# Instance norm over 512 channels: 32 units of 4 MB, sums and normalising on VectorE, squares on ScalarE

## The chip, the cores and the metric

The kernel runs on one core of a Trainium2 chip. The time is device time in microseconds (us), from 12 runs of the kernel before; the profile is of one further execution of it.

## The reference

```python
B, G, C_per_g, H, W = 4, 8, 16, 256, 256      # x float32, gamma (G, C_per_g)
mu = x.mean(axis=(3, 4), keepdims=True)
var = ((x - mu) ** 2).mean(axis=(3, 4), keepdims=True)
x_norm = (x - mu) / np.sqrt(var + 1e-5)
out = x_norm * gamma[None, :, :, None, None]
```

There are 4 x 8 x 16 = 512 channels of 65,536 float32 values. Each channel has its own mean and variance, and one of 128 gamma values. Input and output are 134 MB each, and every value has to be read in before its channel's statistics are known.

## The kernel before

A channel is spread over S = 4 partitions, so the 128 partitions hold 32 channels at a time, a unit of 8 MB; there are U = 16 units. A partition's 16,384 values are cut in NCK = 2 tiles of CW = 8,192 values (128 x 8192 float32, 4 MB). The pool `data` has six such tiles, so three units are resident.

`load(u)` (L47) issues two DMAs on SP's queue, one for each tile. `stats(u)` (L90) runs 32 `bn_stats` on VectorE, each over 512 values of a partition (L94). `finalize(u, st)` (L100) turns them into one scale and one shift for each partition: `bn_aggr` (L102), the mean square (L104), a matmul with the matrix `avg`, which averages over the four partitions of a channel (L109), a copy from PSUM (L114), negated mean and variance (L116, L120), the square root on ScalarE (L125), and then reciprocal, scale and shift on VectorE (L127 to L132). `emit(u, scale, shift)` (L135) normalises each tile in place on ScalarE (L138) and issues its write on ScalarE's own DMA queue (L141).

The order is written out by hand: the program runs under a manual schedule, so each engine takes its instructions as the code lists them. Loads 0, 1 and 2 are issued at the start, as far as the six tiles go. The statistics of units 0 and 1 both stand ahead of the first `finalize`:

```python
    st0 = stats(0)
    for u in range(1, U):
        if u + 1 < U:
            tiles[u + 1] = load(u + 1)
        st = stats(u)
        if u == 1:
            emit(0, *finalize(0, st0))
        emit(u, *finalize(u, st))
```

A load into a tile waits until the write of the unit that held the tile has finished. Loads run on the queue that the profile calls q1 or q10, writes on the other; both use the same 16 DMA engines. Before the loop, `gamma` is loaded on ScalarE's queue (L59), repeated over the partitions of each channel (L75), and brought into columns by four small matmuls (L81, L88).

Of the kernel before, what the change touches and what calls it, by code (L numbers as in the profile page):

```python
# [1 line left out]

# [4 lines left out]

F32 = mybir.dt.float32
ALU = mybir.AluOpType
ACTF = mybir.ActivationFunctionType  # L10


@with_exitstack
def kernel(
    ctx: ExitStack,
    tc: tile.TileContext,
    x: bass.AP,
    gamma: bass.AP,
    out: bass.AP,
):  # L20
    nc = tc.nc
    B, G, C, H, W = x.shape
    P = nc.NUM_PARTITIONS
    HW = H * W
    n_ch = B * G * C
    S = 4
    K = P // S
    F = HW // S
    U = n_ch // K
    CW = 8192  # L30
    NCK = F // CW
    FMAX = 512
    NG = (G * C) // K
    assert HW % S == 0 and F % CW == 0 and (G * C) % K == 0

    xv = x.rearrange("b g c h w -> (b g c h w)").rearrange("(u p f) -> u p f", p=P, f=F)
    ov = out.rearrange("b g c h w -> (b g c h w)").rearrange("(u p f) -> u p f", p=P, f=F)
    gv = gamma.rearrange("g c -> (g c)")

    data = ctx.enter_context(tc.tile_pool(name="data", bufs=3 * NCK))  # L40
    singles = ctx.enter_context(tc.tile_pool(name="singles", bufs=1))
    stats_pool = ctx.enter_context(tc.tile_pool(name="stats", bufs=2))
    psum = ctx.enter_context(tc.tile_pool(name="psum", bufs=2, space=bass.MemoryType.PSUM))

    ctx.enter_context(tc.manual_schedule())

    def load(u):  # L47
        ts = []
        for j in range(NCK):
            t = data.tile([P, CW], F32, name="xt")  # L50
            nc.sync.dma_start(out=t[:], in_=xv[u, :, j * CW : (j + 1) * CW])  # L51
            ts.append(t)
        return ts

    tiles = {0: load(0), 1: load(1)}


    g_row = singles.tile([1, G * C], F32, name="g_row")
    nc.scalar.dma_start(out=g_row[:], in_=gv[None, :])  # L59
    eps_t = singles.tile([P, 1], F32, name="eps_t")  # L60
    nc.vector.memset(eps_t[:], 1e-5)  # L61
    avg = singles.tile([P, K, S], F32, name="avg")
    nc.gpsimd.memset(avg[:], 1.0 / S)  # L63
    nc.gpsimd.affine_select(  # L64
        out=avg[:], in_=avg[:], pattern=[[-S, K], [0, S]], compare_op=ALU.is_ge,
        fill=0.0, base=0, channel_multiplier=1,
    )
    nc.gpsimd.affine_select(  # L68
        out=avg[:], in_=avg[:], pattern=[[S, K], [0, S]], compare_op=ALU.is_ge,
        fill=0.0, base=S - 1, channel_multiplier=-1,  # L70
    )
    one = singles.tile([1, 1], F32, name="one")
    nc.vector.memset(one[:], 1.0)
    g_rep = singles.tile([1, NG, K, S], F32, name="g_rep")
    nc.vector.tensor_copy(  # L75
        out=g_rep[:],
        in_=g_row[:].rearrange("o (n k) -> o n k", n=NG).unsqueeze(3).to_broadcast([1, NG, K, S]),
    )
    g_ps = psum.tile([P, NG], F32, name="g_ps")
    for n in range(NG):  # L80
        nc.tensor.matmul(  # L81
            out=g_ps[:, n : n + 1],
            lhsT=g_rep[:, n].rearrange("o k s -> o (k s)"),
            rhs=one[:],
            start=True, stop=True,
        )
    g_col = singles.tile([P, NG], F32, name="g_col")
    nc.vector.tensor_copy(out=g_col[:], in_=g_ps[:])  # L88

    def stats(u):  # L90
        st = stats_pool.tile([P, F // FMAX, 6], F32, name="st")
        for j in range(NCK):
            for s in range(CW // FMAX):
                nc.vector.bn_stats(  # L94
                    out=st[:, j * (CW // FMAX) + s, :],
                    in_=tiles[u][j][:, s * FMAX : (s + 1) * FMAX],
                )
        return st

    def finalize(u, st):  # L100
        mv = stats_pool.tile([P, 2], F32, name="mv")
        nc.vector.bn_aggr(out=mv[:], in_=st[:].rearrange("p n s -> p (n s)"))  # L102

        nc.vector.scalar_tensor_tensor(  # L104
            out=mv[:, 1:2], in0=mv[:, 0:1], scalar=mv[:, 0:1], in1=mv[:, 1:2],
            op0=ALU.mult, op1=ALU.add,
        )
        ps = psum.tile([P, 2], F32, name="ps")
        nc.tensor.matmul(  # L109
            out=ps[:], lhsT=avg[:].rearrange("p k s -> p (k s)"), rhs=mv[:],  # L110
            start=True, stop=True,
        )
        cm = stats_pool.tile([P, 2], F32, name="cm")
        nc.vector.tensor_copy(out=cm[:], in_=ps[:])  # L114
        nmean = stats_pool.tile([P, 1], F32, name="nmean")
        nc.vector.tensor_scalar(  # L116
            out=nmean[:], in0=cm[:, 0:1], scalar1=-1.0, scalar2=None, op0=ALU.mult,
        )
        var = stats_pool.tile([P, 1], F32, name="var")
        nc.vector.scalar_tensor_tensor(  # L120
            out=var[:], in0=cm[:, 0:1], scalar=nmean[:], in1=cm[:, 1:2],
            op0=ALU.mult, op1=ALU.add,
        )
        std = stats_pool.tile([P, 1], F32, name="std")
        nc.scalar.activation(out=std[:], in_=var[:], func=ACTF.Sqrt, bias=eps_t[:], scale=1.0)  # L125
        rstd = stats_pool.tile([P, 1], F32, name="rstd")
        nc.vector.reciprocal(out=rstd[:], in_=std[:])  # L127
        scale = stats_pool.tile([P, 1], F32, name="scale")
        g = u % NG
        nc.vector.tensor_mul(out=scale[:], in0=rstd[:], in1=g_col[:, g : g + 1])  # L130
        shift = stats_pool.tile([P, 1], F32, name="shift")
        nc.vector.tensor_mul(out=shift[:], in0=nmean[:], in1=scale[:])  # L132
        return scale, shift

    def emit(u, scale, shift):  # L135
        for j in range(NCK):
            t = tiles[u][j]
            nc.scalar.activation(  # L138
                out=t[:], in_=t[:], func=ACTF.Identity, bias=shift[:], scale=scale[:],
            )  # L140
            nc.scalar.dma_start(out=ov[u, :, j * CW : (j + 1) * CW], in_=t[:])  # L141


    st0 = stats(0)
    for u in range(1, U):
        if u + 1 < U:
            tiles[u + 1] = load(u + 1)
        st = stats(u)
        if u == 1:
            emit(0, *finalize(0, st0))  # L150
        emit(u, *finalize(u, st))
        del tiles[u - 1]


# [1 line left out]
_INS = ['x', 'gamma']  # L156
_OUTS = [((4, 8, 16, 256, 256), 'float32')]


# [23 lines left out]
```

## Time and profile before

| what | value |
|---|---|
| median of 12 runs | 634.72 us (634.19 to 635.17) |
| the profiled execution's own time | 635.17 us |
| its span, first to last instruction | 633.5 us |
| VectorE busy | 343.2 us, 54% |
| ScalarE busy | 236.8 us, 37% |
| TensorE busy | 11.2 us, 2% |
| moved by DMA | 268.50 MB, mean 424 GB/s over the span |

The span is what the instructions of the profile cover; the execution's own time lies 1.67 us above it. Busy shares are averages over the whole span. The view of groups gives for each kind of instruction its busy time, the mean of one in ns, and the idle time of its engine just before it with what ended it. A DMA has an issue on a queue, which is short, and a landing, which is later: loads took 26.9 us from issue to landing in the median, writes 50.7 us.

### The profile page before, as it was taken

How to read it: one execution, taken by the hardware profiler on the slowest of the kernel's cores; microseconds unless marked ns; L12 is line 12 of the kernel's file. 1: busy time of each engine (PE TensorE's matmuls, PEld its weight loads, DVE VectorE, ACT ScalarE, POOL GpSimd, SP SyncE). 2: the span in 40 equal slices, each digit the busy share in tenths (PEclk: the TensorE clock that was granted, in tenths of full speed). 3: DMA queues.
4: the chain of work that ended last, by engine and by line, in shares of the span. 5: the costliest groups of instructions: out<-in, count | busy, mean ns of one | idle time of the engine just before them, and what ended most of it. 6: DMA issues, size and time to landing. Idle time of an engine off the chain costs nothing.

```text
span 633.5 us, 972 instructions
## 1 busy us (share of the span) xinstructions
PE 11.2 (2%) x40; PEld 9.8 (2%) x40; DVE 343.2 (54%) x644; ACT 236.8 (37%) x49; POOL 1.4 (0%) x7
## 2 busy tenths in 40 slices
PE   1000000000000000000000000000000000000000
PEld 1000000000000000000000000000000000000000
DVE  2995496454765536664366653467535575354700
ACT  0004959053170622607135080440904408054180
POOL 0000000000000000000000000000000000000000
DMA  9997999999999999999999999999999999999996
GB/s 379 435 441 335 397 424 432 430 430 429 430 435 430 430 430 437 445 435 433 428 430 432 430 435 430 431 432 437 443 432 430 432 432 431 432 432 430 430 430 272
DMA packets 9225, 268.50 MB, mean 424 GB/s; under 512 B 1025, under 2 KB 1026, under 8 KB 1026
## 3 DMA queue, kind: packets, MB, share of 16 engines
q1 hardware_dynamic: 4608, 134.22, 49.3%
q10 hardware_dynamic: 4610, 134.22, 49.3%
q14 instruction: 7, 0.06, 0.0%
HBM read 134.22 MB, written 134.22 MB: 424 GB/s over the span
## 4 chain that ended last, share of the span: by engine, by line
DMA 56%; DVE 20%; another core or an unknown queue 12%; ACT 7%; PE 1%; issue 1%; SPq 0%; ACTq 0%
DMA xt<-in_x_dram 40%; DVE st L94 17%; DMA out_dram<-xt 15%; ACT xt L138 7%; DVE mv L102 2%; PE ps L109 1%; SPq L51 0%; DVE mv L104 0%; ACT std L125 0%; DVE var L120 0%; DVE cm L114 0%; DVE nmean L116 0%; DVE rstd L127 0%; ACTq L141 0%
## 5 line engine op out<-in xcount | busy, mean ns | idle before, releaser
L94 DVE BATCH_NORM_STATS2 st<-xt 128x6 f32<-128x512 f32 x512 | 306.8, 677 | 220.3 <-DMA xt<-in_x_dram 220.1
L138 ACT ACTIVATE xt<-xt,shift,scale 128x8192 f32<-128x8192 f32 x32 | 230.8, 7213 | 16.7 <-DVE shift L132 9.9
L125 ACT ACTIVATE std<-var,eps_t 128x1 f32<-128x1 f32 x16 | 4.7, 294 | 360.5 <-DVE var L120 360.0
L109 PE MATMUL ps<-mv,avg 128*128 128x2 f32 x32 | 9.4, 362 | 585.0 <-DVE mv L104 585.0
L109 PEld LDWEIGHTS ps<-mv,avg 128*128 128x128 f32 x32 | 8.0, 311 | 586.4 <-DVE mv L104 536.7
L102 DVE BATCH_NORM_AGGREGATE mv<-st 128x2 f32<-128x192 f32 x16 | 16.3, 1020 | 0.5
L127 DVE RECIPROCAL rstd<-std 128x1 f32<-128x1 f32 x16 | 2.6, 163 | 18.6 <-ACT std L125 18.6
L114 DVE COPY cm<-ps 128x2 f32<-128x2 f32 x16 | 2.5, 159 | 10.9 <-PE ps L109 10.9
L120 DVE SCALAR_TENSOR_TENSOR var<-cm,nmean 128x1 f32<-128x1 f32 x16 | 3.5, 220 | 0.6
L104 DVE SCALAR_TENSOR_TENSOR mv<-mv 128x1 f32<-128x1 f32 x16 | 3.5, 219 | 0.6
L132 DVE TENSOR_TENSOR shift<-nmean,scale 128x1 f32<-128x1 f32 x16 | 2.6, 160 | 0.6
L130 DVE TENSOR_TENSOR scale<-rstd,g_col 128x1 f32<-128x1 f32 x16 | 2.5, 159 | 0.5
L116 DVE TENSOR_SCALAR nmean<-cm 128x1 f32<-128x1 f32 x16 | 2.5, 154 | 0.6
L81 PE MATMUL g_ps<-one,g_rep 1*128 1x1 f32 x8 | 1.9, 350 | 2.5 <-DVE g_rep L75 2.5
L81 PEld LDWEIGHTS g_ps<-one,g_rep 1*128 1x128 f32 x8 | 1.8, 324 | 2.5 <-DVE g_rep L75 2.5
L125 ACT ACT_TABLE_LOAD x1 | 1.3, 1283 | 1.3 <-PEq L167 1.3
L88 DVE COPY g_col<-g_ps 128x4 f32<-128x4 f32 x1 | 0.2, 163 | 2.0 <-PE g_ps L81 2.0
L75 DVE COPY g_rep<-g_row 1x512 f32<-1x512 f32 x1 | 0.4, 417 | 1.1 <-DMA g_row<-in_gamma_dram 1.1
L61 DVE MEMSET eps_t<- 128x1 f32 x1 | 0.1, 59 | 0.9 <-PEq L167 0.9
L64 POOL TENSOR_SCALAR_AFFINE_SELECT avg<-avg 128x128 f32<-128x128 f32 x1 | 0.5, 517 | 0.1
L68 POOL TENSOR_SCALAR_AFFINE_SELECT avg<-avg 128x128 f32<-128x128 f32 x1 | 0.5, 517 | 0.1
L63 POOL MEMSET avg<- 128x128 f32 x1 | 0.2, 204 | 0.3 <-POOLq L167 0.3
(5 smaller groups left out, 0.5 us busy)
## 6 DMA issues: line engine op xcount, KB each, us to landing
xt<-in_x_dram SPq DMA_DIRECT2D x32, 4096.0 KB, 26.9
out_dram<-xt ACTq DMA_DIRECT2D x32, 4096.0 KB, 50.7
g_row<-in_gamma_dram ACTq DMA_DIRECT2D x1, 0.5 KB
```

The source lines that it names most:

```text
L81: nc.tensor.matmul(out=g_ps[:, n : n + 1], lhsT=g_rep[:, n].rearrange("o k s -> o (k s)"), rhs=one[:], start=True, stop=True,)
L94: nc.vector.bn_stats(out=st[:, j * (CW // FMAX) + s, :], in_=tiles[u][j][:, s * FMAX : (s + 1) * FMAX],)
L102: nc.vector.bn_aggr(out=mv[:], in_=st[:].rearrange("p n s -> p (n s)"))
L104: nc.vector.scalar_tensor_tensor(out=mv[:, 1:2], in0=mv[:, 0:1], scalar=mv[:, 0:1], in1=mv[:, 1:2], op0=ALU.mult, op1=ALU.add,)
L109: nc.tensor.matmul(out=ps[:], lhsT=avg[:].rearrange("p k s -> p (k s)"), rhs=mv[:], start=True, stop=True,)
L114: nc.vector.tensor_copy(out=cm[:], in_=ps[:])
L116: nc.vector.tensor_scalar(out=nmean[:], in0=cm[:, 0:1], scalar1=-1.0, scalar2=None, op0=ALU.mult,)
L120: nc.vector.scalar_tensor_tensor(out=var[:], in0=cm[:, 0:1], scalar=nmean[:], in1=cm[:, 1:2], op0=ALU.mult, op1=ALU.add,)
L125: nc.scalar.activation(out=std[:], in_=var[:], func=ACTF.Sqrt, bias=eps_t[:], scale=1.0)
L127: nc.vector.reciprocal(out=rstd[:], in_=std[:])
L132: nc.vector.tensor_mul(out=shift[:], in0=nmean[:], in1=scale[:])
L138: nc.scalar.activation(out=t[:], in_=t[:], func=ACTF.Identity, bias=shift[:], scale=scale[:],)
```

## The change

The unit becomes 16 channels on 8 partitions each (S = 8), 128 x 8192 values, one tile and one DMA of 4 MB; there are 32 units. Six fixed tiles (`slots`) take the place of the pool, and unit u uses tile u mod 6. All six loads are issued ahead of everything else, with gamma's row after the first, on SP's queue.

For each unit, `reduce_sum` on VectorE sums the tile over its free dimension, and at the same time `Square` on ScalarE with an accumulator output gives the sum of squares; its elementwise output goes as uint8 to a tile `junk` that nobody reads. A matmul with `navg` (entries -1/65536 within a channel) gives minus the mean and minus the mean square in PSUM; VectorE makes the negated variance of these, ScalarE the square root (scale -1, bias eps), and VectorE the reciprocal and its product with gamma. VectorE then normalises the whole tile in place with one `tensor_scalar`, which adds minus the mean, read from PSUM, and multiplies by the scale, read from SBUF. The write is issued on ScalarE's queue, and the load of unit u + 6 on SP's. Gamma's columns are now made after the first unit's sums, by eight small matmuls, since NG is 8 in place of 4.

```diff
-    S = 4
+    S = 8
...
-    data = ctx.enter_context(tc.tile_pool(name="data", bufs=3 * NCK))
+    data = ctx.enter_context(tc.tile_pool(name="data", bufs=1))
...
+    slots = [data.tile([P, F], F32, name=f"xt{i}") for i in range(AHEAD)]
+    def load(u, queue):
+        queue.dma_start(out=slots[u % AHEAD][:], in_=xv[u])
+    g_row = singles.tile([1, G * C], F32, name="g_row")
+    for u in range(AHEAD):
+        load(u, nc.sync)
+        if u == 0:
+            nc.sync.dma_start(out=g_row[:], in_=gv[None, :])
...
+    for u in range(U):
+        t = slots[u % AHEAD]
+        nc.vector.reduce_sum(out=st[:, u, 0:1], in_=t[:], axis=AX.X)
+        square = nc.scalar.activation(
+            out=junk[:], in_=t[:], func=ACTF.Square, accum_out=st[:, u, 1:2],
         )
...
+        if u == 0:
+            gamma_columns()
         ps = psum.tile([P, 2], F32, name="ps")
+        nc.tensor.matmul(out=ps[:], lhsT=navg_w, rhs=st[:, u], start=True, stop=True)
+        nc.vector.tensor_scalar(
+            out=nvar[:, u : u + 1], in0=ps[:, 0:1], scalar1=ps[:, 0:1],
+            scalar2=ps[:, 1:2], op0=ALU.mult, op1=ALU.add,
         )
...
+        nc.scalar.activation(
+            out=std[:, u : u + 1], in_=nvar[:, u : u + 1], func=ACTF.Sqrt,
+            bias=eps_t[:], scale=-1.0,
+        )
+        nc.vector.reciprocal(out=rstd[:, u : u + 1], in_=std[:, u : u + 1])
+        g = u % NG
+        nc.vector.tensor_mul(
+            out=scale[:, u : u + 1], in0=rstd[:, u : u + 1], in1=g_col[:, g : g + 1],
+        )
         nc.vector.tensor_scalar(
+            out=t[:], in0=t[:], scalar1=ps[:, 0:1], scalar2=scale[:, u : u + 1],
+            op0=ALU.add, op1=ALU.mult,
         )
...
+        nc.scalar.dma_start(out=ov[u], in_=t[:])
+        if u + AHEAD < U:
+            load(u + AHEAD, nc.sync)
```

The lines that are taken out are the calls of `stats`, `finalize` and `emit` that were described above.

More of the change, by code (lines that the diff above doesn't have):

```diff
@@ L8 @@
 F32 = mybir.dt.float32
+U8 = mybir.dt.uint8
 ALU = mybir.AluOpType
 ACTF = mybir.ActivationFunctionType
+AX = mybir.AxisListType
 @with_exitstack
@@ L29 @@
     U = n_ch // K
-    CW = 8192
-    NCK = F // CW
-    FMAX = 512
     NG = (G * C) // K
-    assert HW % S == 0 and F % CW == 0 and (G * C) % K == 0
+    AHEAD = 6
+    assert HW % S == 0 and (G * C) % K == 0
     xv = x.rearrange("b g c h w -> (b g c h w)").rearrange("(u p f) -> u p f", p=P, f=F)
@@ L38 @@
     gv = gamma.rearrange("g c -> (g c)")
-    data = ctx.enter_context(tc.tile_pool(name="data", bufs=3 * NCK))
+    data = ctx.enter_context(tc.tile_pool(name="data", bufs=1))
     singles = ctx.enter_context(tc.tile_pool(name="singles", bufs=1))
-    stats_pool = ctx.enter_context(tc.tile_pool(name="stats", bufs=2))
-    psum = ctx.enter_context(tc.tile_pool(name="psum", bufs=2, space=bass.MemoryType.PSUM))
+    psum = ctx.enter_context(tc.tile_pool(name="psum", bufs=4, space=bass.MemoryType.PSUM))
     ctx.enter_context(tc.manual_schedule())
[L47 to L55, printed above, removed]
+    slots = [data.tile([P, F], F32, name=f"xt{i}") for i in range(AHEAD)]
+    def load(u, queue):
+        queue.dma_start(out=slots[u % AHEAD][:], in_=xv[u])
     g_row = singles.tile([1, G * C], F32, name="g_row")
-    nc.scalar.dma_start(out=g_row[:], in_=gv[None, :])
+    for u in range(AHEAD):
+        load(u, nc.sync)
+        if u == 0:
+            nc.sync.dma_start(out=g_row[:], in_=gv[None, :])
     eps_t = singles.tile([P, 1], F32, name="eps_t")
-    nc.vector.memset(eps_t[:], 1e-5)
-    avg = singles.tile([P, K, S], F32, name="avg")
-    nc.gpsimd.memset(avg[:], 1.0 / S)
+    nc.gpsimd.memset(eps_t[:], 1e-5)
+    one = singles.tile([1, 1], F32, name="one")
+    nc.gpsimd.memset(one[:], 1.0)
+    navg = singles.tile([P, K, S], F32, name="navg")
+    nc.gpsimd.memset(navg[:], -1.0 / HW)
     nc.gpsimd.affine_select(
-        out=avg[:], in_=avg[:], pattern=[[-S, K], [0, S]], compare_op=ALU.is_ge,
+        out=navg[:], in_=navg[:], pattern=[[-S, K], [0, S]], compare_op=ALU.is_ge,
         fill=0.0, base=0, channel_multiplier=1,
@@ L68 @@
     nc.gpsimd.affine_select(
-        out=avg[:], in_=avg[:], pattern=[[S, K], [0, S]], compare_op=ALU.is_ge,
+        out=navg[:], in_=navg[:], pattern=[[S, K], [0, S]], compare_op=ALU.is_ge,
         fill=0.0, base=S - 1, channel_multiplier=-1,
     )
-    one = singles.tile([1, 1], F32, name="one")
-    nc.vector.memset(one[:], 1.0)
+    navg_w = navg[:].rearrange("p k s -> p (k s)")
     g_rep = singles.tile([1, NG, K, S], F32, name="g_rep")
[L75 to L85, printed above, removed]
-        )
[L87 to L106, printed above, removed]
-        )
+    g_ps = psum.tile([P, NG], F32, name="g_ps", bufs=1)
+    g_col = singles.tile([P, NG], F32, name="g_col")
+    def gamma_columns():
+        nc.vector.tensor_copy(
+            out=g_rep[:],
+            in_=g_row[:].rearrange("o (n k) -> o n k", n=NG).unsqueeze(3).to_broadcast([1, NG, K, S]),
+        )
+        for n in range(NG):
+            nc.tensor.matmul(
+                out=g_ps[:, n : n + 1],
+                lhsT=g_rep[:, n].rearrange("o k s -> o (k s)"),
+                rhs=one[:],
+                start=True, stop=True,
+            )
+        nc.vector.tensor_copy(out=g_col[:], in_=g_ps[:])
@@ new lines @@
+    junk = singles.tile([P, F], U8, name="junk")
+    st = singles.tile([P, U, 2], F32, name="st")
+    nvar = singles.tile([P, U], F32, name="nvar")
+    std = singles.tile([P, U], F32, name="std")
+    rstd = singles.tile([P, U], F32, name="rstd")
+    scale = singles.tile([P, U], F32, name="scale")
+    squares = []
+    for u in range(U):
[3 more added lines that the diff above has]
+            out=junk[:], in_=t[:], func=ACTF.Square, accum_out=st[:, u, 1:2],
+        )
+        if u:
+            tc.declare_no_dep(square.ins, squares[-1].ins, reason="junk, ordered by the root between")
+        squares.append(square)
+        if u == 0:
+            gamma_columns()
@@ L108, in finalize @@
         ps = psum.tile([P, 2], F32, name="ps")
-        nc.tensor.matmul(
-            out=ps[:], lhsT=avg[:].rearrange("p k s -> p (k s)"), rhs=mv[:],
-            start=True, stop=True,
-        )
-        cm = stats_pool.tile([P, 2], F32, name="cm")
-        nc.vector.tensor_copy(out=cm[:], in_=ps[:])
-        nmean = stats_pool.tile([P, 1], F32, name="nmean")
+        nc.tensor.matmul(out=ps[:], lhsT=navg_w, rhs=st[:, u], start=True, stop=True)
+        nc.vector.tensor_scalar(
+            out=nvar[:, u : u + 1], in0=ps[:, 0:1], scalar1=ps[:, 0:1],
+            scalar2=ps[:, 1:2], op0=ALU.mult, op1=ALU.add,
+        )
@@ L116, in finalize @@
+        nc.scalar.activation(
[6 more added lines that the diff above has]
+            out=scale[:, u : u + 1], in0=rstd[:, u : u + 1], in1=g_col[:, g : g + 1],
+        )
         nc.vector.tensor_scalar(
-            out=nmean[:], in0=cm[:, 0:1], scalar1=-1.0, scalar2=None, op0=ALU.mult,
-        )
@@ L119, in finalize @@
[L119 to L141, printed above, removed]
@@ L144 @@
[L144 to L152, printed above, removed]
+            out=t[:], in0=t[:], scalar1=ps[:, 0:1], scalar2=scale[:, u : u + 1],
+            op0=ALU.add, op1=ALU.mult,
+        )
+        nc.scalar.dma_start(out=ov[u], in_=t[:])
+        if u + AHEAD < U:
+            load(u + AHEAD, nc.sync)
```

## The prediction

> **What bounds the kernel now.** I read the page's second part first, the span in 40 equal slices of 15.8 us, because the kernel only moves 134 MB in and 134 MB out and does little with them.
>
> ```profile
> DMA  9997999999999999999999999999999999999996
> GB/s 379 435 441 335 397 424 432 430 430 429 430 435 430 430 430 437 445 435 433 428 430 432 430 435 430 431 432 437 443 432 430 432 432 431 432 432 430 430 430 272
> ```
>
> The DMA engines are full from end to end, at some 430 GB/s, except in the first slice, in the fourth and fifth, and in the last. So the time is bytes over rate plus a few holes, and a change of the arithmetic is worth only what it does to the holes, unless an engine becomes slower than the transfers. The windows view sizes the holes; its columns are the stretch, its length, the busy time of PE, PEld, DVE, ACT and POOL with instruction counts, PE clock, DMA share, GB/s.
>
> ```profile
> 0.00:4.00 4.00, 1.46 (x7) 1.46 (x8) 0.50 (x3) 1.28 (x1) 1.44 (x7) 1.00 0.71 246
> ...
> 59.00:75.00 16.00, 0.00 (x0) 0.00 (x0) 3.11 (x8) 14.51 (x4) 0.00 (x0) 1.00 0.77 330
> 75.00:160.00 85.00, 1.17 (x4) 1.00 (x4) 50.71 (x94) 41.28 (x8) 0.00 (x0) 1.00 1.00 426
> 160.00:550.00 390.00, 5.88 (x20) 5.02 (x20) 214.75 (x402) 147.20 (x30) 0.00 (x0) 1.00 1.00 433
> ...
> 605.00:608.00 3.00, 0.00 (x0) 0.00 (x0) 0.00 (x0) 2.60 (x1) 0.00 (x0) 1.00 0.86 371
> 608.00:628.00 20.00, 0.00 (x0) 0.00 (x0) 0.00 (x0) 7.21 (x1) 0.00 (x0) 1.00 0.98 421
> 628.00:633.50 5.50, 0.00 (x0) 0.00 (x0) 0.00 (x0) 0.00 (x0) 0.00 (x0) 1.00 0.03 13
> ```
>
> Against 433 GB/s each stretch loses length x (1 - rate/433): 1.7 us in the first 4, 3.8 us from 59 to 75, 1.4 us from 75 to 160, 0.4 us at 605, 0.6 us in the last writes. After 628 nothing of weight moves: 5.5 us until the span ends. The timeline says what the hole near 60 is:
>
> ```profile
> 63.44 0.38 ACTq L141 DMA_DIRECT2D out_dram<-xt  x1
> ...
> 567.91 9.59 DVE L94 BATCH_NORM_STATS2 st<-xt 128x6 f32<-128x512 f32 x16 [6.28 <-DMA xt<-in_x_dram]
> ...
> 587.25 9.59 DVE L94 BATCH_NORM_STATS2 st<-xt 128x6 f32<-128x512 f32 x16 [9.75 <-DMA xt<-in_x_dram]
> ...
> 615.31 0.34 ACTq L141 DMA_DIRECT2D out_dram<-xt  x1
> ```
>
> The first write is issued only at 63.44, when all six buffers are loaded (six tiles need 58 us) and no load may start. The last two loads land 19.34 us apart with writes beside them; one tile of 4.19 MB at 433 GB/s takes 9.7 us, so a load beside a write gets half the engines. The groups give the prices:
>
> ```profile
> L94 DVE BATCH_NORM_STATS2 st<-xt 128x6 f32<-128x512 f32 x512 | 306.8, 677 | 220.3 <-DMA xt<-in_x_dram 220.1
> L138 ACT ACTIVATE xt<-xt,shift,scale 128x8192 f32<-128x8192 f32 x32 | 230.8, 7213 | 16.7 <-DVE shift L132 9.9
> ...
> L109 PE MATMUL ps<-mv,avg 128*128 128x2 f32 x32 | 9.4, 362 | 585.0 <-DVE mv L104 585.0
> ```
>
> and the view of waits, for SP's queue (in total, times, longest):
>
> ```profile
> SPq L51 <- DMA out_dram<-xt: 546.2, 26, 70.9
> ```
>
> VectorE waits 220 us for loads, and the load queue waits 546 us for writes to free a buffer. Both engines have room.
>
> [...]
>
> **The change part by part.** Now per 4 MB unit, 32 of them.
>
> VectorE: one reduce_sum over 8192[...]. The chain after it: matmul 0.60 from DVE's end to its own (54.05 to 54.65), nvar 0.23 as L120, Sqrt 0.33 as L125 with its gap, reciprocal 0.19, scale 0.19, gaps: 1.65 us. Removed are bn_aggr, the mean-square step, the copy of ps, nmean and shift. Then the normalising: 4.4 us[...]. I take 4.4[...], and keep 8.65 for the range. Sum: 14.7 us a unit, 19.0 us at the other end. The DMA pair of a unit (8.39 MB at 433) takes 19.4 us. VectorE stays under, narrowly in the second case.
>
> ScalarE: Square is 7.2 us by L138, plus an accumulator read that no row shows, 0 to 1 us; I take 0.3. It runs beside the reduction; queued behind the previous write's issue (0.34) it ends at 7.9, under 8.65. At nothing, then; without the cover it would cost what it exceeds 8.3.[...] The built program loads a second activation table once, 1.3 us in unit 0.
>
> SP and waits: the load of u+6 waits for the write of u; also for an older load on the same completion semaphore, and the write of 5 and 6 for loads 6 and 7. Behind these on ScalarE stands the next Square, which needs the following tile anyway; behind SP's waits stand only later loads, while others are in the queue. Cost nothing as long as both queues hold work. The gamma row now lies behind load 0 on SP's queue; its copy (1024 elements, 0.8 us by L75's 417 ns for 512), 16 matmul records (1.86 us for 8 before, so 3.7) and a copy, 4.8 us in all, delay unit 0 alone.
>
> The ramp: tile 0 lands at 13.0 as now (first bn_stats 13.02). 13.0 + 8.65 + 4.8 + 1.65 + 4.4 = 32.5 us for the first write, in place of 63.44. By then three of six loads are in, so reads go on and the hole from 59 to 75 (3.8 us) goes. Writes follow every 14.7 us, but beside reads each takes 19.4. The sixth is issued at 32.5 + 5 x 14.7 = 106, when five earlier ones would end at 34 + 97 = 131: 25 us at half rate, 12.5 us of full-rate work, stands ahead. From there VectorE waits for loads, in and out keep equal pace, and this backlog stays.
>
> The end: when the last tile lands, its write is 14.7 + 0.3 + 1.4 (the shortest landing is 11.2 us, less 9.7) = 16.4 us away. In the queue then is the backlog, 12.5, plus unit 30's write, issued 4.7 us earlier at half rate: 9.7 - 2.3 = 7.4. Together 19.9 us, more than 16.4: the engines stay full, and the 0.4 us at 605 goes also. 3.5 us is all the cover; each us beyond it costs one.
>
> Sum against the profiled execution: 633.5 - 3.8 - 0.4 = 629.3 us of span. Its own time was 635.17, 1.67 more than its span; the median is 0.45 under it. Median after: 629.3 + 1.67 - 0.45 = 630.5 us. What is late next is the DMA alone: 268.5 MB at 433 = 620.1, plus 1.7 and 5.5, 627.3 of span (628.5 as a median) if the uneven stretches smooth out as well.
>
> **Rivals.** First, the hole moves to the end: if the backlog does not build, because the queues don't share evenly or the lanes' waits hold writes back, the last unit waits 16.4 - 7.4 = 9 us with idle engines, up to 638.3 + 1.2 = 639.5, typically half, 635. For it: the backlog exists only by my count. Against it: in before the writes take 50.7 us to land against 26.9 for loads, so backlogs of this kind do form.
>
> Second, on the slower side: VectorE becomes the bound[...]. 13.0 + 8.65 + 4.8 + 1.65 + 8.65 = 36.8 for unit 0, 31 x 19.0 = 589 more, then 0.3 + 1.4 + 9.7 + 5.5: 642.7 us of span, 643.9 as a median. It decides from a period of about 18 us, where six units no longer pull far enough ahead.[...]
>
> Third, the new long instructions are dearer than either price: a Square at half rate into uint8 and accumulator (14.2 us) makes a unit 14.2 + 0.3 + 1.65 + 4.4 = 20.6 us, 32 of them some 659, plus 13 and 17: about 689. Nothing in the profile speaks for it.
>
> Fourth, faster still: even rates all through, 628.5.
>
> **How the numbers follow.** Forecast with the fourth case 0.76, moved hole 0.10, VectorE bound 0.09, dear instruction 0.05. About 0.2%, 1.3 us, can be told from no change. Forecast: 0.73 faster, 0.03 same. Moved hole: 0.04, 0.03, 0.03. The others slower. Together 0.77, 0.06, 0.17. The range 627.5 to 637 takes the floor less 1 us for a rate of 434 and most of the moved hole; it leaves the two slow cases out, some 0.17.
>
> **What would show it.** Right: no slice under 420 GB/s but first and last, the first write issued near 33 us, the normalising near 4.4 us and VectorE waiting some 4.7 us a unit for loads, last load landing with over two writes outstanding. Wrong: a normalising of 8.6 us and VectorE over 95% busy; a DMA gap in the last 40 us; Square longer than the reduction; or a middle rate under 430 GB/s, which my count takes as unchanged since each transfer still moves 32 KB pieces per partition, now without gaps between them in memory.

## The result, and the profile after

The changed kernel takes 627.23 us (median of 7 runs, 627.14 to 627.42) against 634.86 for the kernel before, a ratio of 0.9881 (95% interval 0.9872 to 0.989). That is 7.6 us faster where 4.2 were forecast, 0.3 us below the stated range.

The span in 40 slices, now of 15.6 us, from the page of the changed kernel:

```profile
DMA  8999999999999999999999999999999999999998
GB/s 369 436 417 421 436 436 436 436 436 436 434 434 434 434 424 425 434 434 436 436 436 436 434 436 434 430 430 432 425 436 434 436 436 436 436 432 434 434 434 348
```

The weak fourth and fifth slices (335 and 397 before) are gone. Most later slices stand at 434 to 436 where 430 to 432 was common before. The same stretches as in the prediction, from the windows view (columns as there):

```profile
0.00:4.00 4.00, 0.00 (x0) 0.00 (x0) 0.00 (x0) 1.28 (x1) 1.29 (x9) 1.00 0.68 221
...
59.00:75.00 16.00, 0.56 (x2) 0.50 (x2) 14.82 (x6) 7.42 (x3) 0.00 (x0) 1.00 1.02 442
75.00:160.00 85.00, 2.79 (x10) 2.51 (x10) 72.25 (x26) 37.08 (x15) 0.00 (x0) 1.00 1.00 432
160.00:550.00 390.00, 11.18 (x40) 10.04 (x40) 276.95 (x100) 148.33 (x60) 0.00 (x0) 1.00 1.00 433
```

The hole is filled, and the middle runs at 433 GB/s as before. So the gain lies ahead of 160 us and at the end. The groups give what the new instructions cost:

```profile
L101 DVE TENSOR_REDUCE st<-xt 128x1 f32<-128x8192 f32 x32 | 277.9, 8685 | 119.8 <-DMA xt<-in_x_dram 119.8
L102 ACT ACTIVATE junk<-xt 128x8192 uint8<-128x8192 f32 x32 | 224.9, 7030 | 275.5 <-DMA xt<-in_x_dram 243.1
L126 DVE TENSOR_SCALAR xt<-xt,ps,scale 128x8192 f32<-128x8192 f32 x32 | 145.6, 4551 | 1.2
```

The normalising takes 4.55 us, about half of the reduction's 8.69 for as many elements, with its first scalar in PSUM. VectorE still waits 119.8 us for loads, 13.0 of them for the first. The timeline shows the first write and the end:

```profile
33.53 0.38 ACTq L130 DMA_DIRECT2D out_dram<-xt  x1
...
590.47 8.69 DVE L101 TENSOR_REDUCE st<-xt 128x1 f32<-128x8192 f32 x1 [4.33 <-DMA xt<-in_x_dram]
...
600.94 4.55 DVE L126 TENSOR_SCALAR xt<-xt,ps,scale 128x8192 f32<-128x8192 f32 x1
605.52 0.34 ACTq L130 DMA_DIRECT2D out_dram<-xt  x1
```

And the last microseconds of both, in the windows view. First the changed kernel:

```profile
622.00:623.00 1.00, 0.00 (x0) 0.00 (x0) 0.00 (x0) 0.00 (x0) 0.00 (x0) 1.00 0.38 164
623.00:624.00 1.00, 0.00 (x0) 0.00 (x0) 0.00 (x0) 0.00 (x0) 0.00 (x0) 1.00 0.01 0
624.00:625.00 1.00, 0.00 (x0) 0.00 (x0) 0.00 (x0) 0.00 (x0) 0.00 (x0) 1.00 0.00 0
```

Then the kernel before:

```profile
626.00:627.00 1.00, 0.00 (x0) 0.00 (x0) 0.00 (x0) 0.00 (x0) 0.00 (x0) 1.00 1.22 524
627.00:628.00 1.00, 0.00 (x0) 0.00 (x0) 0.00 (x0) 0.00 (x0) 0.00 (x0) 1.00 0.08 33
628.00:629.00 1.00, 0.00 (x0) 0.00 (x0) 0.00 (x0) 0.00 (x0) 0.00 (x0) 1.00 0.01 0
629.00:630.00 1.00, 0.00 (x0) 0.00 (x0) 0.00 (x0) 0.00 (x0) 0.00 (x0) 1.00 0.08 33
630.00:631.00 1.00, 0.00 (x0) 0.00 (x0) 0.00 (x0) 0.00 (x0) 0.00 (x0) 1.00 0.08 33
```

Here is what the prediction read past. 33 GB/s over 1 us is one packet of 32 KB. Up to 631 single packets still follow each other, a DMA share of about one engine in sixteen, while the others are done. The prediction took these microseconds for a fixed tail.

The single DMA records of the trace make this exact. They do not name the DMA engine, but each 4 MB tile has 128 packets of 32 KB and 16 completion packets of 4 bytes, which makes eight and one for each of the 16 engines if they share a tile evenly. In the kernel before, the last three packets of 32 KB start at 627.92, 629.13 and 630.34 us, each as the one ahead of it ends: one engine that is behind. For the last write, in us from the span's start:

| | 15th completion | 16th, the last | lag | from there to the span's end | span |
|---|---|---|---|---|---|
| before | 628.13 | 631.56 | 3.43 | 1.90 | 633.46 |
| after | 623.52 | 623.99 | 0.47 | 1.46 | 625.45 |
| difference | -4.61 | -7.57 | -2.96 | -0.44 | -8.01 |

The fifteenth engine finishes 4.6 us earlier (the middle of the sixteen 5.0), a little more than the forecast's 4.2. The other 3.4 us are one engine that trailed by 3.4 us and now hardly does, and a shorter rest. In the kernel before this lag grows in steps: the spread of the 16 completions of a load is 0.57 us at first, 2.06 by 100 us, 2.50 from 294 us, 3.44 from 412 us, 4.30 from 529 us. Just ahead of the last three steps, at 280, 397 and 523 us, the records have packets of 8 KB that belong to no tile. There are four more: one at 37 us, ahead of a step from 0.57 to 1.51; one at 146 us, after which the spread of the writes rises from 0.70 to 1.33 and that of the loads does not; one at 300 us, which no step follows; and one at 633 us, after the last tile. The page counts them in its third part, in the queue for instructions:

```profile
q14 instruction: 7, 0.06, 0.0%
```

That is the kernel before; this is the changed one:

```profile
q14 instruction: 2, 0.02, 0.0%
```

So the theory, F: while a program runs, its instructions are fetched by DMA, 8 KB at a time, through engines that also move the tiles. Each fetch sets such an engine back, nothing gives the time back as long as all engines are full, and the slowest sets the end. The counts of instructions in the traces fit this: when the packets at 37, 146, 280, 397 and 523 us start, VectorE has begun 46, 177, 311, 432 and 566 instructions, some 130 more each time (121 to 134); at 300 us, where no step follows, it is ScalarE that has begun 63. So too in the changed kernel: the packet at 158 us (VectorE at 49) raises the spread from 0.49 to 1.14 us, the one at 222 us (ScalarE at 61) leaves it as it is. The page counts 644 instructions on VectorE in the kernel before, 512 of them `bn_stats`, and 162 now (the expectations below count a few more, which the page leaves out). The rival, R: the gain beyond the forecast comes from evener transfers, and the instruction count is nothing.

### The profile page after: what moved, and what is told of

Same layout as the page of the kernel before. It is cut to its first block, busy times and chain, and to the rows that moved or that the text cites. A ratio compares the mean times of both kernels' runs of the same rounds, so it can differ in the third digit from the quotient of the medians.

```text
span 625.4 us, 626 instructions
## 1 busy us (share of the span) xinstructions
PE 21.4 (3%) x80; PEld 19.5 (3%) x80; DVE 443.3 (71%) x162; ACT 239.9 (38%) x98; POOL 1.3 (0%) x9
## 4 chain that ended last, share of the span: by engine, by line
DMA 76%; DVE 18%; PE 2%; issue 0%; ACT 0%; SPq 0%; ACTq 0%
DMA xt<-in_x_dram 72%; DVE st L101 15%; DMA out_dram<-xt 5%; DVE xt L126 2%; PE ps L112 1%; PE g_ps L82 1%; DVE nvar L113 0%; ACT L117 0%; ACT std L117 0%; DVE g_rep L77 0%; DVE rstd L121 0%; DVE scale L123 0%; SPq L48 0%; ACTq L117 0%
## 5 line engine op out<-in xcount | busy, mean ns | idle before, releaser
L101 DVE TENSOR_REDUCE st<-xt 128x1 f32<-128x8192 f32 x32 | 277.9, 8685 | 119.8 <-DMA xt<-in_x_dram 119.8
L102 ACT ACTIVATE junk<-xt 128x8192 uint8<-128x8192 f32 x32 | 224.9, 7030 | 275.5 <-DMA xt<-in_x_dram 243.1
L126 DVE TENSOR_SCALAR xt<-xt,ps,scale 128x8192 f32<-128x8192 f32 x32 | 145.6, 4551 | 1.2
L117 ACT ACTIVATE std<-nvar,eps_t 128x1 f32<-128x1 f32 x32 | 9.4, 294 | 77.6 <-DVE nvar L113 77.6
L112 PE MATMUL ps<-st,navg 128*128 128x2 f32 x64 | 17.9, 349 | 556.0 <-DVE st L101 556.0
L112 PEld LDWEIGHTS ps<-st,navg 128*128 128x128 f32 x64 | 16.1, 312 | 557.8 <-issue 557.8
L113 DVE TENSOR_SCALAR nvar<-ps 128x1 f32<-128x1 f32 x32 | 9.2, 288 | 23.4 <-PE ps L112 23.4
L121 DVE RECIPROCAL rstd<-std 128x1 f32<-128x1 f32 x32 | 5.2, 164 | 12.9 <-ACT std L117 12.9
L102 ACT ACTIVATION_READ_ACCUMULATOR junk<-xt 128x1 f32 x32 | 6.0, 186 | 0.0
L123 DVE TENSOR_TENSOR scale<-rstd,g_col 128x1 f32<-128x1 f32 x32 | 5.1, 159 | 1.1
```

Of the source, the lines that this page charges most:

```text
L101: nc.vector.reduce_sum(out=st[:, u, 0:1], in_=t[:], axis=AX.X)
L102: square = nc.scalar.activation(out=junk[:], in_=t[:], func=ACTF.Square, accum_out=st[:, u, 1:2],)
L112: nc.tensor.matmul(out=ps[:], lhsT=navg_w, rhs=st[:, u], start=True, stop=True)
L113: nc.vector.tensor_scalar(out=nvar[:, u : u + 1], in0=ps[:, 0:1], scalar1=ps[:, 0:1], scalar2=ps[:, 1:2], op0=ALU.mult, op1=ALU.add,)
L117: nc.scalar.activation(out=std[:, u : u + 1], in_=nvar[:, u : u + 1], func=ACTF.Sqrt, bias=eps_t[:], scale=-1.0,)
L121: nc.vector.reciprocal(out=rstd[:, u : u + 1], in_=std[:, u : u + 1])
```

## The experiments

**More instructions on VectorE.** Two kernels add short memsets behind each unit's write, 16 in the first kernel and 32 in the second, to a tile `pad` of one element:

```diff
         nc.scalar.dma_start(out=ov[u], in_=t[:])
+        for _ in range(16):
+            nc.vector.memset(pad[:], 0.0)
```

> The changed kernel with 16 memsets of one element behind each unit's write, 512 more instructions on VectorE, which then holds 682 (the kernel before: 652). Theory F (instruction fetch: a block of 8 KB for each 128 instructions or so is fetched by DMA, on one of the 16 DMA engines that also move the tiles, and the slowest engine sets the end): four more fetches, each delays that engine by 0.6 to 0.9 us, so 2.5 to 3.5 us over the changed kernel, about 630.2 us, and the last 4-byte completion packet lands some 3 us behind the other fifteen. Theory R (the gain beyond the forecast comes from even rates, the instruction count is nothing): 627.2 us.

> The same with 32 memsets a unit, 1,024 more on VectorE, some 2 us of its time in each unit, which has over 4 us idle. Theory F: eight more fetches, 5 to 7 us over the changed kernel, about 633 us. Theory R: 627.2 us. If the cost is the engine's time and not the fetches, it also comes in the run with one longer instruction in place of the memsets.

Measured: 630.59 us with 16 (630.41 to 630.67) and 634.86 us with 32 (634.52 to 635.31; ratio to the kernel before 1.0, 0.9991 to 1.0008). So 1,024 instructions of 59 ns on an engine with idle time take the whole gain back. The page of the second kernel, third part:

```profile
q14 instruction: 10, 0.08, 0.0%
```

and its middle and end in the windows view:

```profile
160.00:550.00 390.00, 11.71 (x42) 10.52 (x42) 327.19 (x778) 155.75 (x63) 0.00 (x0) 1.00 1.00 433
...
624.00:626.00 2.00, 0.00 (x0) 0.00 (x0) 0.00 (x0) 0.00 (x0) 0.00 (x0) 1.00 0.08 33
626.00:628.00 2.00, 0.00 (x0) 0.00 (x0) 0.00 (x0) 0.00 (x0) 0.00 (x0) 1.00 0.08 33
628.00:630.00 2.00, 0.00 (x0) 0.00 (x0) 0.00 (x0) 0.00 (x0) 0.00 (x0) 1.00 0.04 16
```

The middle rate is unchanged, the trickle at the end is back and longer. The lag of the last completion is 2.70 us with four more fetches and 5.86 us with eight more, against 0.47. In the second kernel the spread of the 16 completions of a write rises from 0.95 to 8.25 us in eight steps of 0.74 to 0.96 us, each at the first write to finish after a fetch (of its ten fetches, the first lies ahead of the first write and two, at 241.7 and 243.4 us, share a step). R falls. Theory F expected 633 us for the second, 1.9 us too little: it priced a fetch at 0.6 to 0.9 us, and 7.6 us for eight are 0.95 each. A part of these is not lag: the memsets with the gaps between them take 32 x 0.11 = 3.5 us of a unit, VectorE's wait for loads falls from 119.8 to 19.1 us in all, and the first of the last write's 16 completions comes 0.6 us later than in the changed kernel (623.48 and 622.88 us). In the first kernel that is 0.1 us, while the last completion comes 3.3 us later.

**Time in place of instructions.** To part the two, one longer instruction stands where the 16 memsets stood:

```diff
         nc.scalar.dma_start(out=ov[u], in_=t[:])
+        nc.vector.reduce_sum(out=pad[:], in_=t[:, 0:1024], axis=AX.X)
```

> The changed kernel with one more reduction over 1,024 elements behind each unit's write, about 1.1 us of VectorE's time in each unit as with the 16 memsets, but 32 instructions more in place of 512. Theory F: at most one fetch more, 627.2 to 628 us. If VectorE's time is the cause: as with the 16 memsets.

Measured: 628.06 us (627.96 to 628.15), 0.8 us over the changed kernel, in place of 3.4 with the memsets. The groups of the two kernels, first the 16 memsets, then the reduction:

```profile
L133 DVE MEMSET pad<- 1x1 f32 x512 | 30.2, 59 | 26.2
```

```profile
L132 DVE TENSOR_REDUCE pad<-xt 128x1 f32<-128x1024 f32 x32 | 39.0, 1220 | 1.1
```

The reduction took 1.22 us a unit, the 16 memsets 16 x 0.11 = 1.8 with their gaps, so the times are not quite equal. But three fetches stand on the page in place of two, the third at 546 us, and the spread of the completions jumps there from 0.95 to 1.79 us. The lag of the last is 1.06, and the first of the sixteen comes 0.03 us later than in the changed kernel. So the 0.8 us is one fetch, not the engine's time.

**The same number on GpSimd.**

```diff
+        for _ in range(16):
+            nc.gpsimd.memset(pad[:], 0.0)
```

> The changed kernel with 512 memsets of one element on GpSimd, which does nothing else at that time. Theory F, all engines' fetches on one DMA engine: four more fetches, 630 us, as with VectorE. Theory F, each engine's fetches on a DMA engine of its own: the delays don't add to VectorE's, 629 to 629.7 us. Theory R, or VectorE's time as the cause: 627.2 us.

Measured: 628.62 us (628.33 to 628.96), 1.4 us over the changed kernel, with four more fetches as on VectorE and a lag of 1.67 us. That is below both of theory F's figures. Instructions of an idle engine cost too, less than VectorE's (1.4 us for 512, where the same number on VectorE cost 3.4). The four fetches came within the first 86 us, as GpSimd ran ahead at once, and by 128 us the spread of the loads had risen from 0.63 to 4.13 us. The fetch at 163 us, which falls to VectorE by its count (49) and raised the spread in the changed kernel, raised nothing here. So the delays of the two instruction engines did not add, which fits a DMA engine of its own for each, the second form of theory F; the records don't name the engine, so this is not shown directly, nor why the sum is below 629.

**The old kernel with few instructions.** The 8 MB units, the order and the normalising on ScalarE stay; the statistics change, and with them the step to the mean square and the entries of `avg`:

```diff
-            for s in range(CW // FMAX):
-                nc.vector.bn_stats(
-                    out=st[:, j * (CW // FMAX) + s, :],
-                    in_=tiles[u][j][:, s * FMAX : (s + 1) * FMAX],
-                )
+            t = tiles[u][j]
+            nc.vector.reduce_sum(out=st[:, j, 0:1], in_=t[:], axis=AX.X)
+            square = nc.scalar.activation(
+                out=junk[:], in_=t[:], func=ACTF.Square, accum_out=st[:, j, 1:2],
+            )
...
-        nc.vector.bn_aggr(out=mv[:], in_=st[:].rearrange("p n s -> p (n s)"))
...
+        nc.vector.tensor_add(out=mv[:], in0=st[:, 0, :], in1=st[:, 1, :])
```

> The kernel before with its 8 MB units, its order and ScalarE normalising, but the 512 bn_stats replaced by 64 reductions on VectorE and 64 squares on ScalarE, so that VectorE holds 171 instructions in place of 652. The hole stays. Theory F: the trailing completion goes from 3.4 to about 0.5 us, and the last fetch after the work goes too: 2.9 to 3.5 us off, 631.3 to 632 us. Theory R: 634.8 us.

Measured: 628.28 us (628.25 to 628.5), 6.3 us under the kernel before as measured beside it (634.61), twice what was expected. The lag went from 3.43 to 0.15 us and the rest after it from 1.90 to 1.42, 3.8 us together, a little over the 2.9 to 3.5 of theory F. Another 3.1 us came from the hole, which was to stay. Timeline and windows of this kernel:

```profile
60.26 0.38 ACTq L142 DMA_DIRECT2D out_dram<-xt  x1
```

```profile
59.00:75.00 16.00, 0.00 (x0) 0.00 (x0) 6.29 (x4) 14.50 (x4) 0.00 (x0) 1.00 1.04 426
```

The first write left 3.2 us earlier, at 60.26 in place of 63.44 us, just as the six loads ended, and that was most of the hole's width. Of these, 1.2 us are the fourth tile, which was in earlier (42.0 and 43.1; in the kernel before, the fetch at 37 us lies ahead of its landing), 0.9 the shorter last sums of a tile (8.69 and 9.59 us), and the rest `bn_aggr` and the mean-square step. The expectation had not counted this. So 6.3 of the change's 7.6 us come with the new statistics alone; the smaller units, the new order and the normalising on VectorE add about 1 us to that.

**The old kernel with an early first write.**

```diff
-    st0 = stats(0)
+    tiles[2] = load(2)
+    emit(0, *finalize(0, stats(0)))
     for u in range(1, U):
-        if u + 1 < U:
+        if u > 1 and u + 1 < U:
             tiles[u + 1] = load(u + 1)
         st = stats(u)
-        if u == 1:
-            emit(0, *finalize(0, st0))
         emit(u, *finalize(u, st))
```

> The kernel before, but unit 0 is finished and written before the sums of unit 1 are taken; all else as it was. By the forecast the hole from 59 to 75 us goes and nothing more: 3.8 us off, 631.0 us, and the 3.4 us by which the last completion trails the other fifteen stay. If the hole is no loss (the rate makes up for it later): 634.8 us.

Measured: 631.2 us (631.01 to 631.66) against 634.61, ratio 0.9948 (0.9936 to 0.9961). The number is as expected, the way to it is not. Its windows:

```profile
59.00:75.00 16.00, 0.00 (x0) 0.00 (x0) 9.59 (x16) 13.70 (x2) 0.00 (x0) 1.00 1.01 438
```

```profile
602.00:604.00 2.00, 0.00 (x0) 0.00 (x0) 0.00 (x0) 2.00 (x1) 0.00 (x0) 1.00 0.68 295
604.00:606.00 2.00, 0.00 (x0) 0.00 (x0) 0.00 (x0) 2.00 (x1) 0.00 (x0) 1.00 0.08 33
606.00:608.00 2.00, 0.00 (x0) 0.00 (x0) 0.00 (x0) 1.53 (x2) 0.00 (x0) 1.00 0.61 262
```

The hole at 60 us is gone, and one of 3.3 us has opened near 605, while the last unit is normalised and no write is left: the moved hole, the prediction's first rival. It costs little here, because the engine that trailed used it: across the hole the spread of the writes falls from 4.48 to 1.21 us, and the last completion lags by 1.02 us in place of 3.43. Hole and lag did not add in this run: the hole was lost for the engines that were ahead, and the one behind worked through it. In the kernel before, where the stretch at 605 us lost 0.4 us, a lag of 3.43 us showed at the end.

**The slower rival.** The normalising as an operation of two tensor inputs:

```diff
-        nc.vector.tensor_scalar(
-            out=t[:], in0=t[:], scalar1=ps[:, 0:1], scalar2=scale[:, u : u + 1],
+        nc.vector.scalar_tensor_tensor(
+            out=t[:], in0=t[:], scalar=ps[:, 0:1],
+            in1=scale[:, u : u + 1].to_broadcast([P, F]),
             op0=ALU.add, op1=ALU.mult,
         )
```

> The changed kernel with the normalising as an operation of two tensor inputs (the scale repeated along the row)[...], 8.65 us. By the rival of the forecast VectorE becomes the bound: 28.9 + 8.65 for unit 0 from the trace of the changed kernel, 31 periods of 14.93 - 4.55 + 8.65 = 19.03, then 0.3 + 1.4 + 9.7 and 1.4 of tail: 640.3 us of span, 642 us. If the DMA stays the bound: 627.2 us.

Measured: 645.3 us (645.1 to 645.36), ratio to the kernel before 1.0168 (1.0154 to 1.0182). The groups, then the middle and the end in the windows view:

```profile
L126 DVE SCALAR_TENSOR_TENSOR xt<-xt,ps,scale 128x8192 f32<-128x8192 f32 x32 | 280.2, 8757 | 1.1
L101 DVE TENSOR_REDUCE st<-xt 128x1 f32<-128x8192 f32 x32 | 277.7, 8680 | 13.2 <-DMA xt<-in_x_dram 13.2
```

```profile
160.00:550.00 390.00, 11.72 (x42) 10.52 (x42) 365.31 (x105) 148.87 (x63) 0.00 (x0) 1.00 1.00 433
...
605.00:630.00 25.00, 0.56 (x2) 0.50 (x2) 23.82 (x6) 7.42 (x3) 0.00 (x0) 1.00 0.39 168
```

VectorE hardly waits any more; 31 periods of 19.14 us (573.69 to 592.84 in its timeline) make the end. Up to 600 us the DMA rate is the usual one, because the six tiles hold enough work; the price is paid at the end, where the engines run at 168 GB/s, waiting for units one by one. That an operation of two tensor inputs would take 8.65 us was the author's estimate. The expectation's 642 us was 3.3 us low, 0.11 us a period: 8.757 us in place of 8.65, and gaps. It also has a lag of 0.02 us: with room at the end, nothing trailed.

## Why the prediction went wrong, and where it was right

Right, step by step:

- **The bound.** The DMA engines bind before and after; the middle rate is 433 GB/s in both.
- **The hole from 59 to 75 us.** It was to go, 3.8 us, and went. The first write was put at 32.5 us and left at 33.5; the table load of 1.28 us, which the sum for unit 0 had left out, stood on its path.
- **VectorE's unit.** 14.7 us forecast, 14.93 measured (33.41 to 48.34, from the second reduction to the third): 8.69 for 8.65, 4.55 for 4.4, the rest the chain. The wait for loads was (119.8 - 13.0)/25 = 4.3 us a unit where 4.7 was named. The 8.65 and 4.4 us, and 8.65 for a slow normalising, were the author's estimates: the trace of before has neither instruction at this size, and none that takes a scalar from PSUM. Between 4.4 and 8.65 the measured 4.55 us, with the first scalar in PSUM, decide.
- **Square and uint8.** 7.03 us with the uint8 output, where L138 took 7.21 with float32, and 0.19 for the accumulator read; hidden under the reduction.
- **The cover at the end.** The last tile landed by 590.47 and its write was issued 15.05 us later; from 590 to 610 us the mean rate was 441 GB/s, so the backlog of writes covered it. The 3.5 us of margin was a low count: in the records the write ahead of the last ended at 614.3, 7.4 us after the last one could begin (605.5 and 1.4). When the last load had landed, at 590.1 us, three writes were outstanding, as the sign for this has it. The sign "no slice under 420 GB/s" failed by a little: the third slice stands at 417.
- **The slower rival's price.** 643.9 us named, 645.3 measured for an operation of that speed, at 19.1 us a unit. With 32 memsets a unit took 18.5 us where VectorE did not wait, and the first of the last 16 completions came only 0.6 us later; the turn that was named, "about 18 us", agrees with these two and was not tried more closely.

Wrong was one term of the sum: "After 628 nothing of weight moves: 5.5 us until the span ends", which the prediction carried over whole, in the forecast (633.5 - 3.8 - 0.4) and again in the floor of 628.5 us (620.1 plus 1.7 and 5.5). In the kernel before this stretch held about 3.4 us of one trailing DMA engine and 1.9 us of rest. After the change they are 0.5 and 1.5. That is 3.4 of the 3.9 us by which the span was missed (629.3 and 625.45). The prediction gave the instructions on VectorE a price in that engine's time alone, and their number no price at all. The runs with memsets show that the number alone costs: 1,024 instructions bring back 7.6 us at an unchanged rate of the tiles. The run of the old kernel with few instructions shows the other direction, 3.8 us of lag and rest gone. The range's lower end, which rested on that floor, was thereby too high.

A smaller miss is a loss that the prediction listed and left out of its sum: from 75 to 160 us the rate rose from 426 to 432 GB/s, worth 85 x 6/433 = 1.2 us. The first 59 us took 0.7 of this back (246 to 221 GB/s up to 4 us, 430 to 426 from there).

What is left: at eight packets a tile the slowest engine has 512 packets of 32 KB to move, at 1.213 us each (the median record) 621.1 us by estimate, and between the first packet at 1.80 and the last completion at 623.99 us there are 622.2. The lag that remains is 0.47 us; no run was spent on it.

Not settled: why a fetch whose packet takes 0.31 us by its own record sets an engine back by 0.65 to 0.95 us, and which DMA engine a fetch takes.

## What to carry to other kernels

Where DMA is the bound all through, count instructions as well as their time: here each 8 KB of program, some 130 instructions by the counts above, was fetched while the tiles moved and cost 0.8 to 0.95 us at the end for VectorE (one, four and eight fetches more), less for an idle GpSimd (1.4 us for four), and one that falls to ScalarE by its count (222 us in the changed kernel) left the spread as it was. Fewer, longer instructions on an engine that was not the bound were worth 3.8 us of lag and rest in the old kernel, where 171 stood in place of 652 on VectorE, and the third part of the page (the instruction queue) and the last slices at a trickle of one engine show how much. Before a tail is called fixed, ask which engine is still moving in it; and when a hole is removed, look where the next one opens and who catches up in it.

## What the hardware showed that was not expected

- The 16 DMA engines drift apart and stay apart: in the kernel before, the spread between the first and the last completion of a load went from 0.57 to 4.30 us in steps and did not fall again. In the run with an early first write, a hole of 3.3 us near the end brought that of the writes from 4.48 to 1.21 us.
- Fetches of different instruction engines did not add: with 512 memsets on GpSimd, VectorE's fetch at 163 us left a spread of 4.13 us as it was.
- Packets of writes took 1217.6 ns in the mean before and 1213.1 after (4,096 each, the median 1213 in both); these 4.5 ns make 4,096 x 4.5 / 16 = 1.2 us an engine. It is not the fetches: all 18 write packets over 1.3 us in the kernel before lie between 60 and 80 us, at the first writes, and with ten fetches (32 memsets) the mean was 1213.8.
- A `tensor_scalar` of 8,192 float32 with one scalar in PSUM and one in SBUF took 4,551 ns, where the reduction of as many took 8,685.
